# Layer norms whose last sums go through TensorE, with the high part taken from the affine step

## The chip, the cores and the metric

The kernel runs on one core of a Trainium2 chip. The metric is the device time of one execution in microseconds. Three runs of the kernel before took 2368.23, 2368.1 and 3208.11 us, median 2368.23.

## What is computed

The reference is a two-layer encoder over 256 tokens of width 1024. A layer has a mixing part (four mixers on one modulated input, gates, a projection) and an expert part, each closed by a layer norm on the scaled residual plus the gated result:

```python
mod = (c_act @ w_ada[l] + b_ada[l]).reshape(bsz, 6, 1, D_MODEL)
...
h = x * (1.0 + scale1) + shift1
...
mix = jnp.sum(gates * proj, axis=2) @ w_out[l]
x = layer_norm(ALPHA * x + gate1 * mix, ln_g[l, 0], ln_b[l, 0])
h2 = x * (1.0 + scale2) + shift2
y = peer_ffn(h2, p_wq[l], p_subkeys[l], p_u[l], p_v[l])
x = layer_norm(ALPHA * x + gate2 * y, ln_g[l, 1], ln_b[l, 1])
```

There are so four norms in the program: the first and the second norm of each of the two layers. The modulation `mod` is a product of one vector with a 1024 x 6144 matrix per layer.

## The kernel before

Nearly all work is a list of jobs, one per weight tile of 1024 x 128: 70 for the input projection of a layer, 16 for the branches, 8 for the output projection, 16 for the expert queries, 128 each for the two expert tables. SyncE's queue loads a tile (`raw`, three buffers). ScalarE copies it into a high part (`whi`, line 230), VectorE subtracts that from the tile and keeps the low part (`wlo`, line 233). TensorE then makes three matmuls for each of the eight chunks of 128 input features (lines 238 to 240), 24 per job, into a PSUM tile `main`, which rotates over three banks. A tile is split two jobs ahead of its use. Evictions, attention work, the scans of the recurrent mixer and other small work are put between the jobs. The Python code records the work in this order; within it a scheduler decides what stands where on each engine, except for calls through `VB` and `SB`, which stay in the order of the code.

**The norms.** The residual `r` lies feature-major, eight chunks of 128 features x 256 tokens (in the first norm of a layer it is part of the tile `mixA`). A token's mean and variance are sums over the 128 partitions and the eight chunks. `stats` is called for each chunk when it is there: ScalarE squares it (lines 297 and 301), VectorE adds the chunk to a running sum (line 303) and its square to another (line 307). In the first norm the last chunk, in the second the last two, are left out of the running sum and go to TensorE themselves. `norm` then has TensorE multiply each running sum with a column of ones (line 331, tile `lnst`), VectorE works out the mean and the reciprocal root by three Newton steps on two columns (lines 312 to 341), and TensorE spreads the result over all partitions with transposes (line 319, tile `lnb`). VectorE multiplies and adds (line 350) in groups of one or two chunks, one instruction per chunk and operation. `emit` makes the next layer's input of each chunk: an affine step on ScalarE with the norm's and the modulation's factors (`hf`, line 367), its high part by a copy (`hhi`, line 230), its low part on VectorE (`hlo`, line 233). Eight more affine steps on ScalarE (line 372, the folds) bring `r` itself up to date; four of them the scheduler puts between the emits. The norm's successor jobs can't begin before `hhi` and `hlo`. So the first three weight tiles behind a norm (areas) are loaded and split during the jobs before it (`areas_of`), and their 72 matmuls run chunk by chunk as the chunks come. Behind them on TensorE, in the first norms, stands a small product `ssc` (line 881), whose input is the first area job's result, evicted by ScalarE (`qf`, line 1028).

**The end of the expert part.** The second expert table is accumulated in four banks (`vacc`, lines 1084 to 1086), and the last three tiles are held back so that the banks finish one after the other. `take` copies a finished bank to SBUF (ScalarE line 1110, VectorE line 1108), `turn` transposes it on TensorE (`vt`, line 1119), and line 1156 adds it to `r`.

**The modulation.** In layer 0, the 24 halves of 512 KB that the rest of the layer needs are loaded between weight tiles into two rooms in `mixA` (`stage`), and VectorE multiplies and sums each (line 252, `staged`). Job numbers set when: a half is loaded at job 8i/3 and summed three jobs later.

**Scans.** The recurrent mixer works in two directions; each takes a square root on ScalarE (line 662), then gates and scans on VectorE.

## Time and profile before

| | us |
|---|---|
| median of three runs | 2368.23 |
| profiled execution | 2363.6 |
| its span in the trace | 2361.8 |
| TensorE busy | 2289.1 |
| VectorE busy | 1823.6 |
| ScalarE busy | 1262.6 |

The trace holds one execution. Times in its rows count from the start of the span. A row of the timeline gives the start, the time from the first start to the last end, engine, line, operation, destination and sources, shape and, behind an x, how many like instructions in a row it stands for; in square brackets stands how long the engine had been idle and what ended that. Loads of weights into TensorE (PEld) run beside its matmuls (PE). A line with SPq is an entry of SyncE's DMA queue.

### The profile page before, as it was taken

How to read it: one execution, taken by the hardware profiler on the slowest of the kernel's cores; microseconds unless marked ns; L12 is line 12 of the kernel's file. 1: busy time of each engine (PE TensorE's matmuls, PEld its weight loads, DVE VectorE, ACT ScalarE, POOL GpSimd, SP SyncE). 2: the span in 40 equal slices, each digit the busy share in tenths (PEclk: the TensorE clock that was granted, in tenths of full speed). 3: DMA queues.
4: the chain of work that ended last, by engine and by line, in shares of the span. 5: the costliest groups of instructions: out<-in, count | busy, mean ns of one | idle time of the engine just before them, and what ended most of it. 6: DMA issues, size and time to landing. Idle time of an engine off the chain costs nothing.

```text
span 2361.8 us, 43572 instructions
## 1 busy us (share of the span) xinstructions
PE 2289.1 (97%) x16488; PEld 2125.9 (90%) x16488; DVE 1823.6 (77%) x3929; ACT 1262.6 (53%) x2539; POOL 0.2 (0%) x4
## 2 busy tenths in 40 slices
PE   5999999999999999999989999999999999999997
PEld 4998898999999988888889999999999999888886
DVE  7887788998889777777766866889888896665555
ACT  5666546455554454545546765465555545445544
POOL 0000000000000000000000000000000000000000
PEclk9999999999999999999989999999999999999998
DMA  9665454454444577788744454545544445665563
GB/s 357 223 202 203 169 185 171 169 183 165 158 163 160 184 245 274 268 289 294 253 175 157 139 175 154 201 155 173 176 161 161 161 171 199 230 213 194 191 212 108
DMA packets 128033, 461.80 MB, mean 196 GB/s; under 512 B 15440, under 2 KB 20048, under 8 KB 124624
## 3 DMA queue, kind: packets, MB, share of 16 engines
q1 hardware_dynamic: 126816, 453.25, 55.1%
q10 hardware_dynamic: 1008, 5.77, 0.6%
q8 instruction: 131, 2.15, 0.4%
q14 instruction: 78, 0.64, 0.1%
HBM read 450.31 MB, written 5.24 MB: 193 GB/s over the span
## 4 chain that ended last, share of the span: by engine, by line
PE 81%; DVE 10%; DMA 4%; ACT 2%; issue 2%; SPq 0%; ACTq 0%; DVEq 0%
PE main L238 16%; PE main L239 15%; PE main L240 15%; PE vacc L1085 9%; PE vacc L1086 9%; PE vacc L1084 9%; DVE wlo L233 3%; DVE topk L93 2%; PE gw L996 1%; PE gw L997 1%; DMA raw<-in_w_in 1%; DMA mixA<-in_w_ada 1%; DMA adav<-in_w_ada 1%; DVE ada L252 1%; ACT whi L230 1%
## 5 line engine op out<-in xcount | busy, mean ns | idle before, releaser
L233 DVE TENSOR_TENSOR wlo<-raw,whi 128x1024 fp32r<-128x1024 f32 x723 | 879.4, 1218 | 308.3 <-ACT whi L230 305.9
L238 PE MATMUL main<-hhi,wlo 128*128 128x256 f32 x3456 | 1000.4, 290 | 3.7 <-DVE wlo L233 3.1
L240 PE MATMUL main<-hhi,whi 128*128 128x256 f32 x3456 | 978.9, 283 | 0.0
L239 PE MATMUL main<-hlo,whi 128*128 128x256 f32 x3456 | 978.4, 283 | 0.0
L230 ACT ACTIVATE whi<-raw 128x1024 fp32r<-128x1024 f32 x720 | 761.9, 1058 | 402.3 <-PE vacc L1086 278.8
L238 PEld LDWEIGHTS main<-hhi,wlo 128*128 128x128 f32 x3456 | 663.1, 192 | 9.2 <-DVE wlo L233 4.7
L239 PEld LDWEIGHTS main<-hlo,whi 128*128 128x128 f32 x3456 | 663.7, 192 | 0.5
L240 PEld LDWEIGHTS main<-hhi,whi 128*128 128x128 f32 x3456 | 663.1, 192 | 0.1
L1085 PE MATMUL vacc<-wlo,wv 128*128 128x512 f32 x1024 | 398.9, 390 | 0.5 <-DVE wlo L233 0.5
L1084 PE MATMUL vacc<-whi,wv 128*128 128x512 f32 x1024 | 398.6, 390 | 0.0
L1086 PE MATMUL vacc<-whi,wv 128*128 128x512 f32 x1024 | 398.5, 389 | 0.0
L1085 PEld LDWEIGHTS vacc<-wlo,wv 128*128 128x128 f32 x1024 | 192.2, 188 | 41.5 <-DVE wlo L233 1.9
L1084 PEld LDWEIGHTS vacc<-whi,wv 128*128 128x128 f32 x1024 | 192.1, 188 | 40.1 <-ACT whi L230 0.4
L1086 PEld LDWEIGHTS vacc<-whi,wv 128*128 128x128 f32 x1024 | 192.2, 188 | 39.9
L1053 ACT ACTIVATE gel<-main 128x256 f32<-128x256 f32 (+20 forms) x192 | 56.6, 295 | 298.5 <-PE main L240 298.5
L981 DVE TENSOR_TENSOR oha<-ohe,ijg 128x512 f16<-128x512 f16 x256 | 98.5, 420 | 0.9
L252 DVE CUSTOM_DVE_ANT_0 adav<-adav,cact,prm 128x1024 f32<-128x1024 f32 x56 | 71.8, 1283 | 32.4 <-DMA adav<-in_w_ada 31.8
L978 DVE TENSOR_TENSOR ohe<-iota,ijg 128x1024 f16<-128x1024 f16 x128 | 87.3, 683 | 0.2
L1056 DVE TENSOR_TENSOR GB<-GB,gel 128x256 f32<-128x256 f32 (+29 forms) x128 | 46.6, 364 | 45.8 <-ACT gel L1053 44.3
L238 PE MATMUL main<-mixB,wlo 128*128 128x256 f32 x256 | 73.3, 286 | 0.0
L240 PE MATMUL main<-mixB,whi 128*128 128x256 f32 x256 | 72.4, 283 | 0.0
L239 PE MATMUL main<-mixB,whi 128*128 128x256 f32 x256 | 72.4, 283 | 0.0
(233 smaller groups left out, 2215.8 us busy)
## 6 DMA issues: line engine op xcount, KB each, us to landing
raw<-in_p_u SPq DMA_DIRECT2D x256, 512.0 KB, 3.2
raw<-in_p_v SPq DMA_DIRECT2D x256, 512.0 KB, 4.3
raw<-in_w_in SPq DMA_DIRECT2D x134, 512.0 KB, 3.5
adav<-in_w_ada SPq DMA_DIRECT2D x56, 512.0 KB, 5.4
raw<-in_w_br SPq DMA_DIRECT2D x32, 512.0 KB, 3.2
raw<-in_p_wq SPq DMA_DIRECT2D x26, 512.0 KB, 3.3
mixA<-in_w_ada SPq DMA_DIRECT2D x24, 512.0 KB, 4.5
ada<-in_w_ada SPq DMA_DIRECT2D x8, 1024.0 KB, 15.7
```

The costliest lines, as they stand in the source:

```text
L230: return S.activation(hi, src, AF.Copy, scale=scale)
L233: return V.tensor_tensor(lo, src, hi.bitcast(F32), op=OP.subtract)
L238: PE.matmul(out, wlo(c), xhi(c), start=start and c == 0, stop=False)
L239: PE.matmul(out, whi(c), xlo(c), start=False, stop=False)
L240: PE.matmul(out, whi(c), xhi(c), start=False, stop=stop and c == n - 1)
L252: V.tensor_tensor_reduce(out=buf[:, k], in0=buf[:, k], in1=state["cact"], scale=1.0, scalar=prm[:, P_BADA + 48 * l + n:P_BADA + 48 * l + n ...
L978: V.tensor_tensor(flat(eq), iota16.rearrange("p (c k) -> p c k", k=2)[:, None].to_broadcast([128, 2 * NB, 64, 2]), twice(ijg[:, 0:2]), op= ...
L981: V.tensor_tensor(flat(a[:, i:i + 1]), flat(eq[:, 0:1]), ijg[:, 2 + i, :, None, :].to_broadcast([128, NB, 64, 2]), op=OP.mult)
L1053: S.activation(t[:, :n], out[:, :n], AF.Gelu_apprx_tanh)
L1084: PE.matmul(o, wl[:, tt], hi, start=first, stop=False)
L1085: PE.matmul(o, wh[:, tt], lo, start=False, stop=False)
L1086: PE.matmul(o, wh[:, tt], hi, start=False, stop=last)
```

## The change

1. `stats` keeps running sums for the first four chunks alone; chunks 4 to 7 and their squares go to TensorE as they are. The loop over the sums' matmuls now runs over the chunks first, and over sum and square inside.
2. VectorE multiplies and adds chunks 0 and 1 singly and the others in pairs of 128 x 512.
3. `emit` takes the high part from the affine step itself: ScalarE runs that step twice, once into `hhi`, once into `hf`. The folds stay in the order of the code, behind all emits.
4. The last expert bank is finished in two halves of 256 columns, the first copied by VectorE, the second by ScalarE.
5. For the queries' areas the loads are put two jobs earlier (`areas_of` with 2 for 4); splits of areas come two jobs and more behind the loads, where it was one.
6. Both square roots of the scans stay in the order of the code, one right behind the other.
7. Modulation halves are summed five jobs behind their load, where it was three.

```diff
-    def stats(r, m, direct):
+    def stats(r, m, end):
...
-            state["rs"] = [r]
+            state["rs"], state["sqs"] = [r], [state["ss"][:, 1]]
...
-        if m < NC8 - direct:
+        if m < NC8 // 2:
             V.tensor_tensor(ss[:, 0], state["rs"][0], r, op=OP.add)
             state["rs"] = [ss[:, 0]]
+            V.tensor_tensor(ss[:, 1], ss[:, 1], sq, op=OP.add)
         else:
             state["rs"].append(r)
-        state["stats_end"] = V.tensor_tensor(ss[:, 1], ss[:, 1], sq, op=OP.add)
+            state["sqs"].append(sq)
+        state["stats_end"] = end
...
-        for i, xs in enumerate((state["rs"], [state["ss"][:, 1]])):
-            for k, x in enumerate(xs):
+        n = len(state["rs"])
+        for k in range(n):
+            for i, xs in enumerate((state["rs"], state["sqs"])):
...
-        for ms in ((0,), (1, 2), (3, 4), (5, 6), (7,)):
+        for m0, m1 in ((0, 1), (1, 2), (2, 4), (4, 6), (6, 8)):
             for i, op in enumerate((OP.mult, OP.add)):
-                for m in ms:
-                    V.tensor_tensor(r[:, m], r[:, m], b[i], op=op)
-            for m in ms:
+                V.tensor_tensor(r[:, m0:m1], r[:, m0:m1], b[i][:, None].to_broadcast([128, m1 - m0, T]), op=op)
+            for m in range(m0, m1):
                 emit(m)
...
-            S.activation(h, r[:, m], AF.Identity, scale=fold[:, 0, 0, m:m + 1], bias=fold[:, 0, 1, m:m + 1])
-            marks["hi"] = split_hi(hi[:, m], h)
+            for a in (hi[:, m], h):
+                marks["hi"] = S.activation(a, r[:, m], AF.Identity, scale=fold[:, 0, 0, m:m + 1], bias=fold[:, 0, 1, m:m + 1])
...
-            S.activation(r[:, m], r[:, m], AF.Identity, scale=fold[:, 1, 0, m:m + 1], bias=fold[:, 1, 1, m:m + 1])
+            SB.activation(r[:, m], r[:, m], AF.Identity, scale=fold[:, 1, 0, m:m + 1], bias=fold[:, 1, 1, m:m + 1])
...
-            before[n + 1 + i].hooks.append(lambda i=i, j=j: area_split(i, j))
+            before[n + 2 + i].hooks.append(lambda i=i, j=j: area_split(i, j))
...
-                S.activation(tr, tr, AF.Sqrt)
+                SB.activation(tr, tr, AF.Sqrt)
...
-            w[8 * i // 3 + 3].hooks.append(lambda i=i: staged(i))
+            w[8 * i // 3 + 5].hooks.append(lambda i=i: staged(i))
...
-        areas_of(jobs[-16:], outs, 4)
+        areas_of(jobs[-16:], outs, 2)
...
-                        for i, x in enumerate(held):
-                            three(b, *x, False, i == VLAST - 1)
-                        take(b)
-                        if b:
-                            turn(b - 1)
+                        for part in ((0, 512),) if b < 3 else ((0, 256), (256, 256)):
+                            for i, x in enumerate(held):
+                                three(b, *x, False, i == VLAST - 1, *part)
+                            take(b, *part)
+                            if b and part[0] == 0:
+                                turn(b - 1)
                     turn(3)
```

On TensorE, at the first norm of layer 0, stands between the last output job's matmuls (`main0`) and the transposes of the result, before:

```order
L239 MATMUL main0_4260<-hlo_3403,whi_4188 128x256
L240 MATMUL main0_4260<-hhi_3402,whi_4188 128x256
L331 MATMUL lnst7_4303<-ones_87,lnss_4035 128x1 x2
L331 MATMUL lnst7_4303<-ones_87,mixA_241 128x1 x2
L331 MATMUL lnst7_4303<-ones_87,lnss_4035 128x1 x2
L319 MATMUL lnb6_4330<-cst_82,rs_4316 128x128 x2
```

and with the change, down to the sum and the square of chunk 4; the last two rows then stand three more times, for chunks 5 to 7:

```order
L239 MATMUL main0_4254<-hlo_3402,whi_4188 128x256
L240 MATMUL main0_4254<-hhi_3401,whi_4188 128x256
L334 MATMUL lnst7_4296<-ones_87,lnss_4035 128x1 x4
L334 MATMUL lnst7_4296<-ones_87,mixA_241 128x1 x2
L334 MATMUL lnst7_4296<-ones_87,sq_4186 128x1 x2
```

Six matmuls of the program have become twenty, all of them still behind the last output job. The first square's product stands third, ahead of all chunks' own.

On VectorE, at the second norm of layer 0, from the first sum that needs the last expert bank (`vt6`, `vt0` are its transposes, `lnss` the running sums) to the first rows that no longer belong to the sums, before:

```order
L1156 SCALAR_TENSOR_TENSOR r2_13314<-vt6_13695,gq_13705,r2_13314 128x256
L307 TENSOR_TENSOR lnss_13708<-lnss_13708,sq_13721 128x256
L303 TENSOR_TENSOR lnss_13708<-lnss_13708,r2_13314 128x256
L307 TENSOR_TENSOR lnss_13708<-lnss_13708,sq_13726 128x256
L1156 SCALAR_TENSOR_TENSOR r2_13314<-vt6_13695,gq_13705,r2_13314 128x256
L1156 SCALAR_TENSOR_TENSOR r2_13314<-vt0_13696,gq_13705,r2_13314 128x256
L303 TENSOR_TENSOR lnss_13708<-lnss_13708,r2_13314 128x256
L307 TENSOR_TENSOR lnss_13708<-lnss_13708,sq_13731 128x256
L1156 SCALAR_TENSOR_TENSOR r2_13314<-vt0_13696,gq_13705,r2_13314 128x256
L307 TENSOR_TENSOR lnss_13708<-lnss_13708,sq_13736 128x256
L434 MEMSET mixA_13849 128x4x2
L435 MEMSET mixA_13849 128x4
```

and with the change:

```order
L1158 SCALAR_TENSOR_TENSOR r2_13315<-vt6_13696,gq_13716,r2_13315 128x256
L303 TENSOR_TENSOR lnss_13719<-lnss_13719,r2_13315 128x256
L1158 SCALAR_TENSOR_TENSOR r2_13315<-vt6_13696,gq_13716,r2_13315 128x256
L305 TENSOR_TENSOR lnss_13719<-lnss_13719,sq_13722 128x256
L1158 SCALAR_TENSOR_TENSOR r2_13315<-vt0_13697,gq_13716,r2_13315 128x256
L305 TENSOR_TENSOR lnss_13719<-lnss_13719,sq_13727 128x256
L1158 SCALAR_TENSOR_TENSOR r2_13315<-vt0_13697,gq_13716,r2_13315 128x256
L305 TENSOR_TENSOR lnss_13719<-lnss_13719,sq_13732 128x256
L233 TENSOR_TENSOR wlo_13757<-raw_13595,whi_13756 128x512
L337 TENSOR_SCALAR lnw_13783<-lnst7_13762 128x2
```

Of seven plain adds (the seventh follows behind the two clears) four are left; three of these are for the squares of chunks 1 to 3, of which the first stood ahead of these rows before.

On ScalarE, at the first norm of layer 0, the last chunks' emits, the folds of `mixA` and the first evictions of the area jobs (`qf`), before:

```order
L367 ACTIVATE hf<-mixA,fold 128x256
L372 ACTIVATE mixA<-mixA,fold 128x256
L230 ACTIVATE hhi<-hf 128x256
L372 ACTIVATE mixA<-mixA,fold 128x256 x4
L1028 ACTIVATE qf<-main_4396 128x256
L373 DMA xd<-mixA 128x2048
```

and with the change:

```order
L370 ACTIVATE hhi<-mixA,fold 128x256
L370 ACTIVATE hf<-mixA,fold 128x256
L93 ACTIVATE mixA<-mixA,fold 128x256 x8
L1029 ACTIVATE qf<-main_4397 128x256
L375 DMA xd<-mixA 128x2048
L1029 ACTIVATE qf<-main_4424 128x256
```

All eight folds (line 93 is that of the helper that keeps the order) are now between the last emit and the first eviction; before, four stood among the emits. The copy into `hhi` is an affine step.

## Rows read from the trace of the kernel before

**Rows 1.** The page: busy time, share of the span, instructions.

```profile
PE 2289.1 (97%) x16488; PEld 2125.9 (90%) x16488; DVE 1823.6 (77%) x3929; ACT 1262.6 (53%) x2539; POOL 0.2 (0%) x4
```

**Rows 2.** Waits of TensorE: total us, times, longest.

```profile
PE lnst L331 <- DVE lnss L303: 5.3, 2, 2.9
...
PE z L652 <- DVE mixA L478: 2.7, 1, 2.7
```

**Rows 3.** Waits of VectorE.

```profile
DVE mixA L252 <- DMA mixA<-in_w_ada: 22.1, 13, 4.3
```

**Rows 4.** Busy time by window: length, engines, PEclk (granted clock), DMA share, GB/s.

```profile
60.00:310.00 250.00, 240.94 (x1907) 225.92 (x1906) 193.27 (x428) 151.72 (x315) 0.00 (x0) 0.99 0.57 198
1220.00:1470.00 250.00, 249.06 (x2018) 235.97 (x2017) 175.01 (x389) 157.69 (x321) 0.00 (x0) 1.00 0.48 163
...
270.00:280.00 10.00, 7.20 (x43) 7.00 (x42) 8.57 (x22) 5.11 (x14) 0.00 (x0) 0.76 0.44 159
```

**Rows 5.** Timeline of a late modulation half in layer 0: SyncE's queue, VectorE, TensorE.

```profile
262.60 1.40 SPq L247 DMA_DIRECT2D mixA<-in_w_ada  x1
...
268.61 1.28 DVE L252 CUSTOM_DVE_ANT_0 mixA<-mixA,cact,prm 128x1024 f32<-128x1024 f32 x1 [4.35 <-DMA mixA<-in_w_ada]
...
275.12 0.96 PE L620 MATMUL stc<-ones,sqc 128*128 128x1 f32 x4 [2.80 <-ACT sqc L616]
```

**Rows 6.** Timeline of TensorE, first norm of layer 0: the sums' matmuls.

```profile
373.34 0.51 PE L331 MATMUL lnst<-ones,lnss 128*128 128x1 f32 x4
...
375.05 0.61 PE L331 MATMUL lnst<-ones,lnss 128*128 128x1 f32 x4 [0.36 <-DVE lnss L307]
```

**Rows 7.** The same, second norm of layer 0.

```profile
1194.42 1.84 PE L331 MATMUL lnst<-ones,r 128*128 128x1 f32 x8
1196.13 0.99 PE L331 MATMUL lnst<-ones,lnss 128*128 128x1 f32 x4
```

**Rows 8.** Busy time by window around the two second norms' sums.

```profile
1193.00:1194.00 1.00, 0.45 (x3) 0.46 (x3) 1.00 (x4) 0.64 (x2) 0.00 (x0) 0.69 0.97 410
...
2346.00:2347.00 1.00, 0.88 (x8) 0.79 (x8) 0.87 (x3) 0.42 (x2) 0.00 (x0) 1.00 0.05 16
2347.00:2348.00 1.00, 0.92 (x6) 0.83 (x5) 0.85 (x2) 0.38 (x1) 0.00 (x0) 0.55 0.00 0
```

**Rows 9.** Groups of ScalarE in 380 to 391: count, busy us, mean ns, idle before.

```profile
L367 ACT ACTIVATE hf<-mixA,fold 128x256 f32<-128x256 f32 x8 | 4.5, 588 | 5.9 <-DVE mixA L350 5.9
L372 ACT ACTIVATE mixA<-mixA,fold 128x256 f32<-128x256 f32 x8 | 4.4, 587 | 0.0
L230 ACT ACTIVATE hhi<-hf 128x256 fp32r<-128x256 f32 x8 | 3.0, 403 | 0.0
```

**Rows 10.** Timeline behind the first norm of layer 0: first affine step, first eviction, ssc.

```profile
380.42 0.60 ACT L367 ACTIVATE hf<-mixA,fold 128x256 f32<-128x256 f32 x1 [5.88 <-DVE mixA L350]
...
390.90 0.36 ACT L1028 ACTIVATE qf<-main 128x256 f32<-128x256 f32 x1
...
391.52 0.61 PE L881 MATMUL ssc<-subk,qf 128*128 128x128 f32 x4
```

**Rows 11.** Timeline of the second norm of layer 0: scaled and plain adds, first eviction, fourth job.

```profile
1186.88 1.66 DVE L1156 SCALAR_TENSOR_TENSOR r<-vt,gq,r 128x256 f32<-128x256 f32 x4 [2.05 <-PE vt L1119]
...
1190.89 0.48 DVE L1156 SCALAR_TENSOR_TENSOR r<-vt,gq,r 128x256 f32<-128x256 f32 x1
...
1194.76 0.42 DVE L307 TENSOR_TENSOR lnss<-lnss,sq 128x256 f32<-128x256 f32 x1 [0.18 <-ACT sq L301]
...
1212.76 0.38 ACT L687 ACTIVATE mixA<-main 128x256 f32<-128x256 f32 x1 [0.24 <-PE main L240]
...
1213.52 0.28 PE L238 MATMUL main<-hhi,wlo 128*128 128x256 f32 x1
```

**Rows 12.** Timeline of the last norm: VectorE's last adds, the last sums' matmuls.

```profile
2347.02 0.96 DVE L307 TENSOR_TENSOR lnss<-lnss,sq 128x256 f32<-128x256 f32 x2 [0.15 <-ACT sq L301]
...
2348.04 1.01 PE L331 MATMUL lnst<-ones,lnss 128*128 128x1 f32 x4
```

More of the change, by code (lines that the diff above doesn't have):

```diff
@@ L327, in norm @@
         stp = bank(7, [128, 2, 2], name="lnst")
-        for i, xs in enumerate((state["rs"], [state["ss"][:, 1]])):
-            for k, x in enumerate(xs):
+        n = len(state["rs"])
+        for k in range(n):
+            for i, xs in enumerate((state["rs"], state["sqs"])):
                 for t in range(2):
-                    PE.matmul(stp[:, i, t:t + 1], x[:, t * 128:(t + 1) * 128], ones, start=i == k == t == 0, stop=k == len(xs) - 1,
+                    PE.matmul(stp[:, i, t:t + 1], xs[k][:, t * 128:(t + 1) * 128], ones, start=i == k == t == 0, stop=k == n - 1,
                               skip_group_check=True)
@@ L805, in post @@
                 r = state["r"][:, m]
-                V.scalar_tensor_tensor(r, out, mods[l][:, 16 + m:17 + m], r, op0=OP.mult, op1=OP.add)
-                stats(r, m, 1)
+                stats(r, m, V.scalar_tensor_tensor(r, out, mods[l][:, 16 + m:17 + m], r, op0=OP.mult, op1=OP.add))
             return Job(src=A["w_out"][l, m], mm=mm, post=post)
@@ L1077, in pre, with three @@
                 state["wv", j] = w[:, 0], w[:, 1]
-            def three(b, hi, lo, wh, wl, first, last):
-                o = state["acc4"][b]
+            def three(b, hi, lo, wh, wl, first, last, o0=0, n=512):
+                o = state["acc4"][b][:, o0:o0 + n]
                 tt = slice(b % 2 * 128, b % 2 * 128 + 128)
-                hi, lo = (x.rearrange("p c m -> p (c m)")[:, b // 2 * 512:b // 2 * 512 + 512] for x in (hi, lo))
-                PE.matmul(o, wl[:, tt], hi, start=first, stop=False)
-                PE.matmul(o, wh[:, tt], lo, start=False, stop=False)
-                PE.matmul(o, wh[:, tt], hi, start=False, stop=last)
+                hi, lo = (x.rearrange("p c m -> p (c m)")[:, b // 2 * 512 + o0:b // 2 * 512 + o0 + n] for x in (hi, lo))
+                PE.matmul(o, wl[:, tt], hi, start=first, stop=False, skip_group_check=o0 > 0)
+                PE.matmul(o, wh[:, tt], lo, start=False, stop=False, skip_group_check=o0 > 0)
+                PE.matmul(o, wh[:, tt], hi, start=False, stop=last, skip_group_check=o0 > 0)
             def mm(hi, lo):
@@ L1103, in layer, with take @@
         held = []
-        def take(b):
-            out = state["raws"][:, NAREA * D + 512 * b:NAREA * D + 512 * (b + 1)]
-            if b % 2:
-                V.tensor_copy(out, state["acc4"][b])
+        def take(b, o0, n):
+            out, acc = state["raws"][:, NAREA * D + 512 * b + o0:NAREA * D + 512 * b + o0 + n], state["acc4"][b][:, o0:o0 + n]
+            if b % 2 and o0 == 0:
+                V.tensor_copy(out, acc)
             else:
-                S.activation(out, state["acc4"][b], AF.Copy)
+                S.activation(out, acc, AF.Copy)
         def turn(b):
@@ L1155, in ln2 @@
             for m in range(NC8):
-                V.scalar_tensor_tensor(r[:, m], state["turned", m // 4][m % 4 // 2][:, m % 2], gq[:, m:m + 1], r[:, m],
-                                       op0=OP.mult, op1=OP.add)
-                stats(r[:, m], m, 2)
+                stats(r[:, m], m, V.scalar_tensor_tensor(r[:, m], state["turned", m // 4][m % 4 // 2][:, m % 2], gq[:, m:m + 1],
+                                                         r[:, m], op0=OP.mult, op1=OP.add))
             g, b = pv(P_LNG + 16 * l + 8, 8), pv(P_LNB + 16 * l + 8, 8)
```

## Prediction

> **What bounds the kernel now.** I read the page first: TensorE is busy for 97% of the span [rows 1], so an edit on another engine moves the time only where TensorE waits for that engine. Next the list of waits, sorted by engine. For TensorE it names the norms (the sums' matmuls wait 5.3 us for VectorE's adds, in two places) and the mixing of layer 0 (z waits 2.7 us) [rows 2]; for VectorE it names a DMA wait of 22.1 us in front of the modulation sums [rows 3]. The third view is busy time by window. It shows what these mixing waits are worth, because layer 1 runs the same mixing jobs without modulation sums: of 250 us TensorE is busy for 240.94 in layer 0 and for 249.06 in layer 1 [rows 4], so 8.1 us more stand idle in layer 0. Then the timeline of the places that the change touches. The median of the runs before is 2368.2 us and the profiled execution took 2363.6; I work out a difference in the profiled execution and add it to the median.
>
> **Part one: sums in the norms.** Before, the sums' matmuls come in two places at the layer-0 first norm: four at 373.34, when the last output job's matmuls are just done, and the last four from 375.05 on, ending at 375.66 (375.05 + 0.61) [rows 6]. Between them TensorE waits for VectorE. One matmul of the program is two on the chip (six make twelve). Four take 0.51, of which the last is 0.17 long: (0.51 - 0.17) / 3 = 0.11 us from one to the next, though each has a single column. The change makes 20 of the program, 40 on the chip, and the order puts all of them behind the last job's matmuls. 39 x 0.11 + 0.2 = 4.5 us from 373.34 is 377.8: 2.2 us later than now. VectorE's two adds that are saved were worth less than the matmuls that replace them. The first norm of layer 1 is laid out in the same way: 2.2 again.
>
> In the second norms VectorE was the limit: behind the last bank's transposes stand four scaled adds and seven plain adds, from 1190.89 to 1195.18 (1194.76 + 0.42) [rows 11]. In the new order four of each stand there. Four scaled adds take 1.66 [rows 11], about 0.41 each; a plain add starts about 0.34 after its predecessor in the same stretch ((1195.18 - 1190.89 - 1.66 - 0.3 of a wait and two clears) / 7). The bank's first half is ready before the second and feeds the first two scaled adds, so I let them start at about 1190.1. That gives 1190.1 + 1.66 + 4 x 0.34 = 1193.1 (0.8 later if they start as now). But the last of VectorE's adds gates the fifth of 40 matmuls: 36 are still to come. What these take hangs on TensorE's clock. At full clock 36 x 0.11 = 4.0, end 1197.1: no change against now (1196.13 + 0.99 = 1197.12) [rows 7]. At half clock eight took 1.84 [rows 7], 0.21 from one to the next: 7.7, end 1200.9, +3.8. The granted clock fell to 1.2 GHz between 1193 and 1194 (0.69 of full as a mean), with TensorE less than half busy; in the last norm it fell at about 2347.1, with these one-column matmuls in flight [rows 8]. So I expect the fall about a microsecond into the run: 8 at 0.11, 28 at 0.21, end about 1200.2, +3.1. In the last norm, by the same steps, the adds end at about 2345.8 in place of 2347.98 (2347.02 + 0.96), and 10 at 0.11 with 26 at 0.21 end at 2352.6 against 2349.05 [rows 12]: +3.5 (+0.8 at full clock).
>
> A rule speaks to that. Rows 7 and 8 show eight and then four sums' matmuls back to back at half clock, and no rise. The Trainium skill (TensorE: Matmul & The Clock Gate, section "What's actually happening") says that the slow clock is the default and "activity releases the throttle"; a longer run of matmuls might then keep the clock up. By the rows the two second norms cost 3.1 and 3.5; by the rule they would cost 0 and 0.8. No row here has 40 of them in one run, so the rule is a rival below.
>
> **Part two: the high part straight from the affine step, folds behind.** The first high chunk comes 0.4 us earlier, one ScalarE copy less. But ScalarE's total grows. Before: eight affine steps, eight copies, eight folds, which fill 10.48 us from 380.42 to the query eviction at 390.90 that TensorE's next matmuls (ssc, 391.52) need [rows 10]. A copy is 0.403 long against 0.588 for an affine step or fold [rows 9]. The change turns the eight copies into affine steps: 8 x 0.18 = 1.4 us more. The paired adds of VectorE bring chunk 2 some 0.4 later than now, when two single adds would do. So the eviction comes about 1.75 later, and TensorE stood at it with next to no slack (the eviction ends at 391.26, ssc starts at 391.52). Putting the folds last doesn't help, since the eviction stands behind all eight in either order. With 0.1 to 0.3 of slack I take +1.5 in each first norm. In layer 0's second norm the first eviction (1212.76) was just in time for the fourth job at 1213.52 [rows 11]; ScalarE was free 0.24 earlier, at 1212.52; with the folds 1.75 later the eviction ends at 1212.52 + 1.75 + 0.38 = 1214.65: +1.1. The last norm has no such step; pairs save VectorE about 0.5 there.
>
> **Part three: last bank in halves.** Twice nine matmuls of half the width cost TensorE about the same; the second half waits for VectorE's copy of the first, which mostly lies beside the four transposes placed between. It is in the 1190.1 above; alone 0 to +0.3.
>
> **Part four: areas' loads two places earlier, splits one later.** The weights arrive long before their use either way; 0, since no row shows TensorE waiting for a raw load here. If that cover failed, one load's landing would show, once per layer.
>
> **Part five: both square roots in a row.** Fewer table loads on ScalarE (18 in the new order, 22 before), beside TensorE's matmuls: 0. The first direction's scan work moves later into the gate jobs, where VectorE has more to do: 0 to +2, I take +1 in layer 0 and 0 in layer 1.
>
> **Part six: modulation sums two jobs later.** At 262.60 a half is loaded, at 268.61 VectorE has waited 4.35 us for it, and TensorE's stc at 275.12 waits 2.80 [rows 5]; the granted clock over 270 to 280 is 0.76 [rows 4], so about 4.8 us ran at half clock, worth 2.4. With z's 2.7 [rows 2] that is 7.9 from below the counter. Two jobs are about 5.8 us, more than the longest wait. From both sides: 0, if the waits come back elsewhere, and 8.1 + 2.4 = 10.5, if all of layer 0's idle time goes. I take 6.5, since the scans and the first jobs also make some of the idle time.
>
> **Sum.** First norms 2 x (2.2 + 1.5) = 7.4; second norm of layer 0 3.1 + 1.1 = 4.2; last norm 3.5 - 0.5 = 3.0; scans +1; modulation sums -6.5. Together +9.1, so 2372.7 in the profiled execution and 2377 as a median.
>
> **Rivals.** First, the clock stays up through the sums: the second norms cost 1.1 and 0.3 in place of 4.2 and 3.0, the sum is +3.3: 2371.5. For it: in the last norm eight of the sums' matmuls ran at full clock before it fell. Against it: in layer 0 the clock was down before the second eight began. Second, the later sums remove nothing, since a half's next load now stands on SyncE's queue behind the sum of the half before it in two jobs of three, and raw weight loads queue behind that: +15.6, 2384. Against it: at 262.60 the load was issued only 1.65 us before VectorE came to the sum (268.61 - 4.35), so VectorE is ahead of the queue and the new wait is mostly met already. Third, on the other side: the DMA waits of VectorE count in full, because in layer 0 the mixing is a chain through VectorE and each wait pushes all that follows. Then 22.1 [rows 3] goes and the sum is 7.4 + 4.2 + 3.0 + 1 - 22.1 = -6.5: 2361.7, not slower. It decides as soon as the mixing gives more than the 15.6 that the rest costs. Against it: only 8.1 us more are idle in layer 0 than in layer 1 [rows 4].
>
> **How the numbers follow.** The forecast 0.5 (its own range 2372 to 2383), the clock that stays up 0.2, sums that give nothing 0.15, the full gain of the mixing 0.1; 0.05 for what I don't see. The range of 8 in 10 reaches from the third rival to a little beyond the second: 2362 to 2387. A measurement of this kernel tells about 2% from no change, 47 us here; no case comes near that on either side, so within 2% gets 0.97, slower 0.02, faster 0.01.
>
> **What would show it.** In the profile after: 40 sums' matmuls per norm; the first broadcast of the layer-0 first norm 2 us later behind the last output job; the first query eviction 3.5 to 4 us later behind that job, with a TensorE wait for ssc of over a microsecond; the second norms' sums at 0.21 from one to the next for most of the run; no VectorE wait of over 2 us for a modulation half. I am wrong if the sums' matmuls run closer than 0.11, if they begin before the last job's end, if ScalarE is not what the job behind the areas waits for, or if layer 0's mixing gains more than 10 us or nothing.

## The result and the profile after

The changed kernel took 2379.71 us as a median of five runs (2378.36 to 2383.85). The kernel before took 2363.14 to 2368.23 us in four of five runs; the fifth, of 3208 us, is left aside. The ratio is 1.0064 with an interval of 1.0053 to 1.0075, so the change costs 12 to 18 us. The prediction was 2377 us, with +9.1 over the kernel before; it added this to 2368.2 us, and the four runs here have a median of 2366.2. The profiled execution took 2379.28 us, 15.7 more than the profiled one of before.

VectorE's wait for the sums' matmuls in the kernel before (total, times, longest):

```profile
DVE lnw L334 <- PE lnst L331: 2.5, 2, 1.4
```

The page and the waits of the changed kernel, beside [rows 1 to 3]:

```profile
PE 2307.4 (97%) x16610; PEld 2145.1 (90%) x16610; DVE 1810.9 (76%) x3879; ACT 1262.4 (53%) x2537; POOL 0.2 (0%) x4
```

```profile
PE main L238 <- DVE wlo L233: 7.2, 8, 2.4
...
PE ssc L882 <- ACT qf L1029: 1.9, 2, 1.2
PE lnst L334 <- DVE lnss L305: 1.6, 1, 1.6
...
DVE lnw L337 <- PE lnst L334: 19.8, 4, 6.6
...
DVE mixA L252 <- DMA mixA<-in_w_ada: 17.4, 10, 4.2
```

TensorE's wait for the sums' adds has shrunk from 5.3 us to 1.6; VectorE's wait for the sums' matmuls has grown from 2.5 us to 19.8. The wait has changed sides. A wait of `ssc` for ScalarE is new, and the wait for modulation halves is 17.4 us in 10 places, where it was 22.1 in 13 [rows 3].

The timeline at the first norm of layer 0, TensorE and ScalarE, to be read beside [rows 6, 10]. The first broadcast before:

```profile
378.51 1.12 PE L319 MATMUL lnb<-cst,rs 128*128 128x128 f32 x4 [2.86 <-DVE rs L316]
```

and the changed kernel:

```profile
369.49 0.95 PE L334 MATMUL lnst<-ones,lnss 128*128 128x1 f32 x8
...
373.43 0.58 PE L334 MATMUL lnst<-ones,sq 128*128 128x1 f32 x4
376.86 1.11 PE L321 MATMUL lnb<-cst,rs 128*128 128x128 f32 x4 [2.85 <-DVE rs L318]
...
387.09 4.04 ACT L93 ACTIVATE mixA<-mixA,fold 128x256 f32<-128x256 f32 x8
391.03 0.36 ACT L1029 ACTIVATE qf<-main 128x256 f32<-128x256 f32 x1
...
391.44 0.71 PE L882 MATMUL ssc<-subk,qf 128*128 128x128 f32 x4 [0.65 <-ACT qf L1029]
```

From the first sums' matmul to the broadcast it is 376.86 - 369.49 = 7.37 us; before, 378.51 - 373.34 = 5.17. All eight folds stand in front of the eviction, and TensorE waits for it: it begins 391.03 - 376.86 = 14.17 us behind the broadcast, before 390.90 - 378.51 = 12.39.

The second norm of layer 0, timeline and windows, beside [rows 7, 8]:

```profile
1192.53 0.61 PE L334 MATMUL lnst<-ones,lnss 128*128 128x1 f32 x4 [1.57 <-DVE lnss L305]
...
1198.63 0.99 PE L334 MATMUL lnst<-ones,sq 128*128 128x1 f32 x4
```

```profile
1192.00:1193.00 1.00, 0.47 (x5) 0.47 (x5) 1.00 (x3) 0.42 (x1) 0.00 (x0) 1.00 0.84 352
1193.00:1194.00 1.00, 1.00 (x9) 1.00 (x8) 0.07 (x1) 0.00 (x0) 0.00 (x0) 0.69 1.04 442
1194.00:1200.00 6.00, 5.62 (x27) 5.53 (x26) 0.34 (x5) 0.00 (x0) 0.00 (x0) 0.50 0.48 199
```

The 36 matmuls behind VectorE's last add begin at 1192.53; the clock falls to 1.2 GHz a microsecond later and stays there, with TensorE busy for 5.62 of 6 us.

One stretch was not in the forecast, the first jobs of layer 1. `wblk` is a weight tile of the mixing that is loaded there; its entry follows that of the residual's store 3.9 to 4.2 us later in every trace. Before:

```profile
1216.71 0.33 SPq L432 DMA_DIRECT2D wblk<-in_d_w  x1
1217.13 2.41 SPq L1199 DMA_DIRECT2D raw<-in_w_in  x3
...
1222.89 1.06 ACT L230 ACTIVATE whi<-raw 128x1024 fp32r<-128x1024 f32 x1 [3.02 <-DMA raw<-in_w_in]
```

After:

```profile
1217.11 0.39 PE L238 MATMUL main<-hhi,wlo 128*128 128x256 f32 x1 [0.49 <-ACT mixA L689]
...
1220.80 0.33 SPq L434 DMA_DIRECT2D wblk<-in_d_w  x1
1221.21 2.86 SPq L1200 DMA_DIRECT2D raw<-in_w_in  x3
...
1228.85 1.06 ACT L230 ACTIVATE whi<-raw 128x1024 fp32r<-128x1024 f32 x1 [5.29 <-DMA raw<-in_w_in]
...
1231.22 0.58 PE L238 MATMUL main<-hhi,wlo 128*128 128x256 f32 x1 [2.32 <-DVE wlo L233]
```

Raw loads stand on SyncE's queue behind that of `wblk`, which stands behind the residual's store, and the store waits for the folds. Counted from the start of TensorE's fourth job (1213.52 before [rows 11], 1217.11 now), the three raw loads are issued 3.6 us later before and 4.1 now; the copy of the first follows 5.8 us behind the issue before and 7.6 now, and TensorE stood still for 2.3 us. So the late folds account for about 0.5 us of the delay, and the loads' own time for 1.9.

The stretches below are worked out from the starts of the first instruction of each group in seven traces (one execution each): the kernel before, the changed one, and experiments that follow. "Fourth job" is the first TensorE work behind the 72 area matmuls.

| stretch, us | before | changed | e1 | e2 | e5 | e7 | e9 |
|---|---|---|---|---|---|---|---|
| mixing, layer 0 | 356.1 | 352.4 | 356.8 | 360.0 | 357.7 | 352.1 | 354.1 |
| norm 1: sums to broadcast | 5.2 | 7.4 | 5.3 | 7.6 | 5.2 | 5.2 | 5.2 |
| broadcast to fourth job | 13.0 | 14.6 | 14.6 | 13.4 | 14.2 | 14.2 | 12.4 |
| norm 2: first transposes to broadcast | 16.1 | 19.6 | 15.9 | 19.8 | 16.1 | 15.9 | 15.4 |
| broadcast to fourth job | 13.5 | 14.5 | 14.6 | 13.7 | 13.1 | 13.2 | 12.4 |
| mixing, layer 1 | 313.6 | 317.2 | 314.0 | 312.8 | 313.6 | 313.1 | 312.7 |
| norm 1, layer 1: sums to broadcast | 5.2 | 7.9 | 5.2 | 7.4 | 5.2 | 5.3 | 5.3 |
| broadcast to fourth job | 13.0 | 14.6 | 14.6 | 14.0 | 14.3 | 14.5 | 12.4 |
| last norm: first transposes to broadcast | 15.5 | 18.7 | 16.4 | 15.9 | 15.8 | 16.3 | 16.0 |

The mixing of layer 0 shows how far single executions can be trusted: the changed kernel, e1 and e2 run the same code there and differ by 7.6 us. The stretch from a broadcast to the fourth job varies too: e5, e11 and e12, with the emits of before, took 13.1 to 14.4 us there, where the trace of before has 13.0 to 13.5. The last norm varies with the clock: e2 has the sums of the changed kernel and took 15.9 us in place of 18.7, and e6 took 16.1.

### The profile page after: what moved, and what is told of

The parts are those of the page before. It is cut to its first block, busy times and chain, and to the rows that moved or that the text cites. A ratio compares the mean times of both kernels' runs of the same rounds, so it can differ in the third digit from the quotient of the medians.

```text
span 2377.4 us, 43769 instructions
## 1 busy us (share of the span) xinstructions
PE 2307.4 (97%) x16610; PEld 2145.1 (90%) x16610; DVE 1810.9 (76%) x3879; ACT 1262.4 (53%) x2537; POOL 0.2 (0%) x4
## 4 chain that ended last, share of the span: by engine, by line
PE 87%; DVE 6%; ACT 3%; DMA 3%; issue 1%; SPq 0%; ACTq 0%; DVEq 0%
PE main L238 17%; PE main L239 17%; PE main L240 17%; PE vacc L1085 10%; PE vacc L1087 10%; PE vacc L1086 10%; DVE wlo L233 2%; PE gw L997 1%; DMA mixA<-in_w_ada 1%; PE gw L998 1%; PE lnst L334 1%; DVE ada L252 1%; PE ssc L882 1%; PE pt L507 1%; DMA raw<-in_w_in 1%
## 5 line engine op out<-in xcount | busy, mean ns | idle before, releaser
L238 PEld LDWEIGHTS main<-hhi,wlo 128*128 128x128 f32 x3456 | 664.7, 192 | 14.5 <-DVE wlo L233 9.3
L1085 PE MATMUL vacc<-whi,wv 128*128 128x512 f32 (+1 forms) x1030 | 400.2, 389 | 0.2
L1086 PE MATMUL vacc<-wlo,wv 128*128 128x512 f32 (+1 forms) x1030 | 400.0, 388 | 0.0
L1087 PE MATMUL vacc<-whi,wv 128*128 128x512 f32 (+1 forms) x1030 | 399.8, 388 | 0.0
```

The source lines that it names most:

```text
L238: PE.matmul(out, wlo(c), xhi(c), start=start and c == 0, stop=False)
L1085: PE.matmul(o, wl[:, tt], hi, start=first, stop=False, skip_group_check=o0 > 0)
L1086: PE.matmul(o, wh[:, tt], lo, start=False, stop=False, skip_group_check=o0 > 0)
L1087: PE.matmul(o, wh[:, tt], hi, start=False, stop=last, skip_group_check=o0 > 0)
```

## The experiments

Each ratio is to runs of the kernel before on the same chip. Where a run is set against the changed kernel or another experiment, it is by medians. The changed kernel was timed apart from all experiments, and e5 to e8 on another chip than e1 to e4 and e9 to e12; so the difference of the two ratios is given where it tells another story.

**e1, the first part taken back.**

```diff
-        if m < NC8 // 2:
+        if m < NC8 - direct:
...
-            state["sqs"].append(sq)
+        state["stats_end"] = V.tensor_tensor(ss[:, 1], ss[:, 1], sq, op=OP.add)
```

> The changed kernel with its first part taken back: running sums on VectorE for all but one chunk in the first norms and all but two in the second, squares all on VectorE, 12 and 16 sums' matmuls on the chip. Theory: the 40 matmuls cost 2.2 and 2.7 us in the first norms, 3.5 in layer 0's second and 3.2 in the last, 11.6 together, and come back in full; about 2368 median, 0.995 of the changed kernel, and about 4 us above the fast runs of the kernel before. Rival: VectorE's saved adds were worth something and the loss lies in the emits and what follows; then under 5 us come back (2375 or more).

Measured: 2367.84 us, ratio 1.0003 (0.9989 to 1.0017): 11.9 us below the changed kernel. The three stretches from sums or transposes to broadcast that belong to layers 0 and 1 are back at 5.3, 15.9 and 5.2. The sums' matmuls are the greatest part of the loss; by the two ratios it is 14 us.

**e2, folds on VectorE.**

```diff
-            SB.activation(r[:, m], r[:, m], AF.Identity, scale=fold[:, 1, 0, m:m + 1], bias=fold[:, 1, 1, m:m + 1])
+            V.tensor_scalar(r[:, m], r[:, m], fold[:, 1, 0, m:m + 1], fold[:, 1, 1, m:m + 1], op0=OP.mult, op1=OP.add)
```

> The changed kernel with the eight folds on VectorE in place of ScalarE. Theory: the late folds hold the first eviction in each norm (0.5 to 0.8 us of TensorE's wait) and, in layer 0's second norm, the store of the residual, behind which the room of wblk and with it the raw loads of layer 1 wait (2.3 us of wait and about 1.7 by the clock that falls); both go: about 4 to 6 us less than the changed kernel, 2374 to 2376, and no wait of TensorE for wlo at the start of layer 1. Rival: the stall at the start of layer 1 comes from another thing (the splits of the areas one job later); then it stays and 1 to 2 us are saved.

Measured: 2374.48 us, ratio 1.0035 (1.0025 to 1.0046): 5.2 us below the changed kernel. The wait for `ssc` is gone in both first norms, and so is the one at the start of layer 1: the store comes 11.1 us behind the broadcast in place of 14.3, and in SyncE's queue a raw load now stands ahead of `wblk`.

```profile
1222.79 0.33 SPq L1200 DMA_DIRECT2D raw<-in_w_in  x1
1225.45 0.33 SPq L434 DMA_DIRECT2D wblk<-in_d_w  x1
1226.74 3.21 SPq L1200 DMA_DIRECT2D raw<-in_w_in  x2
```

So the folds on ScalarE held back `ssc`. For the start of layer 1 this run doesn't show the cause, because the loads stand in another order; e6 bears on it. The splits of the areas, one job later in this kernel too, don't make the stall by themselves.

**e3, the sums twice.** The second set goes into columns that nobody reads.

```diff
+        for k in range(n):
+            for i, xs in enumerate((state["rs"], state["sqs"])):
+                for t in range(2):
+                    PE.matmul(stp[:, 2 + i, t:t + 1], xs[k][:, t * 128:(t + 1) * 128], ones, start=False, stop=k == n - 1,
...
```

> The changed kernel with every norm's 40 sums' matmuls issued a second time into columns of the same bank that nobody reads. Theory: a sums' matmul costs 0.11 us at full and 0.21 at half clock and does not bring the clock back; the first norms cost between 4.5 (all at full) and 8.5 more each, the second norms 8.5 more each: 26 to 34 us, 2405 to 2414. Rival (a long run of matmuls keeps or brings the clock up): 4.5 each or less, since the first 40 would be faster too: 18 us or less, 2398 or less.

Measured: 2414.32 us, 34.6 above the changed kernel, just over the theory's end. Timeline and windows of the first norm of layer 0:

```profile
374.63 0.58 PE L334 MATMUL lnst<-ones,mixA 128*128 128x1 f32 x4
...
378.49 1.84 PE L339 MATMUL lnst<-ones,lnss 128*128 128x1 f32 x8
...
384.46 0.99 PE L339 MATMUL lnst<-ones,sq 128*128 128x1 f32 x4
```

```profile
374.00:378.00 4.00, 4.00 (x37) 4.00 (x38) 1.08 (x2) 0.42 (x1) 0.00 (x0) 0.99 0.02 4
378.00:380.00 2.00, 2.00 (x12) 2.00 (x11) 0.00 (x0) 0.00 (x0) 0.00 (x0) 0.50 0.00 0
380.00:382.00 2.00, 2.00 (x11) 2.00 (x11) 0.00 (x0) 0.00 (x0) 0.00 (x0) 0.50 0.00 0
382.00:386.00 4.00, 4.00 (x21) 4.00 (x20) 0.00 (x0) 0.00 (x0) 0.00 (x0) 0.50 0.00 0
```

Eighty one-column matmuls run back to back; TensorE is busy in every slice, and yet the clock falls to half after about the first forty and does not come back. The Trainium skill (TensorE: Matmul & The Clock Gate, section "What's actually happening") says that activity releases the throttle; this trace doesn't agree for one-column matmuls, and the measurement decides. Here a long run of sums neither kept the clock up nor brought it back, against the first rival of the prediction. But the fall doesn't come at the same place each time. In the last norm of e2, with the 40 sums from 2357.36 on, the clock held for most of the run:

```profile
2359.00:2361.00 2.00, 2.00 (x20) 2.00 (x19) 0.21 (x1) 0.72 (x2) 0.00 (x0) 1.00 0.03 8
2361.00:2363.00 2.00, 1.60 (x9) 1.51 (x9) 0.33 (x3) 0.00 (x0) 0.00 (x0) 0.54 0.00 0
```

That norm took 15.9 us there, 0.4 more than before, in place of the changed kernel's 3.2 more. So for single norms the rival can come true.

**e4, running sums last.**

```diff
-        for k in range(n):
+        for k in [*range(1, n), 0]:
```

> The changed kernel with the sums' matmuls in another order: the four late chunks and their squares first, the two running sums last. Theory: in the second norms 36 of 40 matmuls stood behind VectorE's last add; now 24 to 28 of them run while VectorE works, and the sums end 3 to 5 us earlier there; the first norms stay, as TensorE comes to them late: 6 to 9 us less than the changed kernel, 2371 to 2374. Rival (the number of matmuls at half clock decides, not what they wait for): under 2 us.

Measured: 2378.35 us, ratio 1.0056 (1.0033 to 1.0079), 1.4 below the changed kernel: a miss. In layer 0's second norm the stretch from the transposes to the broadcast fell from 19.6 to 16.7, as expected. In the last norm it stayed at 19.1: the sums now wait for the first late chunk itself,

```profile
2355.99 0.60 PE L334 MATMUL lnst<-ones,r 128*128 128x1 f32 x4 [1.48 <-DVE r L1158]
```

and the clock fell about a microsecond after, so nearly all ran at half speed. The first norm of layer 0 lost what the second gained: from the first sum to the broadcast it took 9.1 us in place of 7.4, with the granted clock at 0.50 from 374 on, in the middle of its sums. So what the order saves is less than what hangs on the moment at which the clock falls.

**e5, only the later modulation sums, on the kernel before.**

```diff
-            w[8 * i // 3 + 3].hooks.append(lambda i=i: staged(i))
+            w[8 * i // 3 + 5].hooks.append(lambda i=i: staged(i))
```

> The kernel before with one edit: the modulation halves of layer 0 summed five jobs behind their load in place of three. Theory (the prediction's): layer 0's mixing loses its waits, 4 to 6.5 us less than the kernel before, ratio 0.9973 to 0.9983. Rival (the second of the prediction): a later sum only makes the next load of the same room later, VectorE waits as often, and the time is that of the kernel before within 2 us, ratio 0.999 to 1.001. In the profile the two differ in VectorE's wait for halves: under 8 us against about 17 to 22.

Measured: ratio 0.9987 (0.9977 to 0.9997); medians 2364.77 and 2367.72 us. The gain is about 3 us, half of what the prediction took. VectorE waits for halves just as often:

```profile
DVE mixA L252 <- DMA mixA<-in_w_ada: 21.3, 12, 4.0
```

The trace shows why, and it is not the rival's reason. Here is the half of [rows 5] in this run, SyncE's queue and VectorE:

```profile
265.92 0.43 SPq L247 DMA_DIRECT2D mixA<-in_w_ada  x1
...
271.59 1.28 DVE L252 CUSTOM_DVE_ANT_0 mixA<-mixA,cact,prm 128x1024 f32<-128x1024 f32 x1 [4.02 <-DMA mixA<-in_w_ada]
```

The sum begins 5.7 us behind the issue of its load; before, it was 268.61 - 262.60 = 6.0. It has not moved. Counted by the tile splits (`wlo`) that stand ahead of it on VectorE, 23 of the 24 sums are where they were in the kernel before; only the fourth, at 85.7 before and 93.9 here, is one split further back. SyncE's queue has the same order in both traces. So the edit changed the job numbers in the Python code, and the scheduler put nearly all sums back where they had stood. The rooms were not the limit either: a load is issued 4.7 us or more after the sum that frees its room, in both traces. Where the 3 us come from is open: layer 0's mixing in the one trace is not shorter than before.

**e6, the emits as before**, on the changed kernel: `hhi` copied from `hf`, folds placed by the scheduler.

```diff
-            for a in (hi[:, m], h):
-                marks["hi"] = S.activation(a, r[:, m], AF.Identity, scale=fold[:, 0, 0, m:m + 1], bias=fold[:, 0, 1, m:m + 1])
+            S.activation(h, r[:, m], AF.Identity, scale=fold[:, 0, 0, m:m + 1], bias=fold[:, 0, 1, m:m + 1])
+            marks["hi"] = split_hi(hi[:, m], h)
...
-            SB.activation(r[:, m], r[:, m], AF.Identity, scale=fold[:, 1, 0, m:m + 1], bias=fold[:, 1, 1, m:m + 1])
+            S.activation(r[:, m], r[:, m], AF.Identity, scale=fold[:, 1, 0, m:m + 1], bias=fold[:, 1, 1, m:m + 1])
```

> The changed kernel with the third part taken back: the high part is copied from the affine step's result, and the scheduler places the folds. Theory: ScalarE's longer work behind the norms cost 1.6 us in each first norm, about 1 in layer 0's second and up to 3.6 at the start of layer 1, where raw loads stand behind a room that the stored residual frees: 4 to 7 us less than the changed kernel, about 2374, much as with the folds on VectorE. Rival: the first high chunk's 0.5 us is worth as much as the longer chain costs; then it is within 2 us of the changed kernel.

Measured: 2380.44 us, ratio 1.0046 (1.0033 to 1.0059). By medians that is 0.7 us above the changed kernel, as the rival had it; by the ratios it is 4 below, as the theory had it. The six runs spread from 2374.52 to 2386.50, so this doesn't decide. In its trace the fourth job comes without a wait for ScalarE, but the first area matmul comes 3.35 us after the broadcast, where it was 2.50, so a part of what is saved behind is spent in front.

The start of layer 1 is of more use. The store stands 12.6 us behind the broadcast again (before 12.7, changed 14.3), and the raw loads are issued 3.3 us behind the start of the fourth job. Yet TensorE stood still:

```profile
1229.58 3.25 SPq L1200 DMA_DIRECT2D raw<-in_w_in  x3
...
1238.08 1.06 ACT L230 ACTIVATE whi<-raw 128x1024 fp32r<-128x1024 f32 x1 [5.45 <-DMA raw<-in_w_in]
...
1240.45 0.58 PE L238 MATMUL main<-hhi,wlo 128*128 128x256 f32 x1 [2.48 <-DVE wlo L233]
```

The copy came 8.5 us after the issue. In e1, with the folds late, it came 5.8 us after, and TensorE's wait was 0.5 us. So the late folds are not what makes the stall large; the time of the loads is.

**e7, sums as before and folds on VectorE**: the diffs of e1 and e2 together.

> The changed kernel with the first part taken back (running sums on VectorE as before) and the folds on VectorE. Theory: both gains add, 11.9 and 5.2 us, since one lies ahead of the broadcast and the other behind it: about 2362.6, 0.998 to 0.999 of the kernel before. Rival: with VectorE free of folds again or the sums back, VectorE's queue delays the low parts; then 2366 or more.

Measured: 2363.63 us, ratio 0.9982 (0.9973 to 0.9991). The two gains add to 16 of the expected 17 us, and this is 4 us faster than the kernel before.

**e8, squares of the last chunks to TensorE as well**, on e7: 16 matmuls in the first norms, 24 in the second.

```diff
-        state["stats_end"] = V.tensor_tensor(ss[:, 1], ss[:, 1], sq, op=OP.add)
+            state["stats_end"] = V.tensor_tensor(ss[:, 1], ss[:, 1], sq, op=OP.add)
         else:
             state["rs"].append(r)
+            state["sqs"].append(sq)
```

> As the run before, but the chunks that the kernel before left out of the running sum (one in the first norms, two in the second) go to TensorE with their squares, 16 and 24 matmuls; in the second norms the running sums come last. Theory: one plain add less stands behind the last chunk and few matmuls are added, 0.5 us less in each first norm and about 1 in each second one: 2 to 3 us below the run before. Rival: 8 more matmuls at half clock cost the second norms 1.7 us each, no gain.

Measured: 2366.71 us, ratio 0.9999 (0.9990 to 1.0008), 3 above e7 in the same series: the rival. In the traces the two second norms, with eight matmuls more each, took 17.0 and 18.4 us from the first transposes to the broadcast, in e7 15.9 and 16.3. Even eight more of these matmuls cost what the saved adds bring and more.

**e9, idle TensorE filled around the norms**, on e7. The matmuls go into a bank that nobody reads.

```diff
+                PE.matmul(out, a[:, 0], a.rearrange("p c m -> p (c m)")[:, :512], start=True, stop=True)
...
+        warm(12, last_sum)
...
+        warm(8, last_b)
...
+            if b == 3:
+                warm(8, last_t)
```

> The fastest kernel so far (sums as before, folds on VectorE) with idle TensorE filled around the first three norms: 8 matmuls of 512 columns on area weights into an unread bank behind the last transposes of layer 0's second norm, 12 behind the sums of each norm, 8 behind each broadcast. Theory: behind a norm 72 matmuls take 10.7 to 11.9 us, of which 8.6 (72 at 0.12) is full clock; if TensorE never stands still the clock stays at 2.4 GHz, the areas take about 9, the broadcast 0.5 less and 16 sums' matmuls of layer 0's second norm 1.6 less: 7 to 10 us below that kernel, about 2355, 0.995 of the kernel before. Rival: the chain of affine steps and low parts paces the areas anyway; then under 3 us.

Measured: 2359.94 us, ratio 0.9977 (0.9964 to 0.9989). That is 3.7 below e7 by medians, but e7 was timed on another chip, and by the ratios it is 1 us, with intervals that overlap; a gain over e7 is not shown. Windows at the first norm, e7:

```profile
378.00:380.00 2.00, 1.94 (x9) 1.95 (x10) 2.00 (x5) 1.62 (x4) 0.00 (x0) 0.50 0.02 6
380.00:382.00 2.00, 2.00 (x11) 2.00 (x11) 2.00 (x6) 2.00 (x5) 0.00 (x0) 0.50 0.00 0
```

and e9, windows and timeline:

```profile
375.00:379.00 4.00, 3.98 (x20) 2.78 (x19) 3.83 (x15) 0.90 (x2) 0.00 (x0) 1.00 0.21 48
379.00:389.00 10.00, 9.35 (x75) 8.94 (x75) 9.74 (x24) 8.80 (x18) 0.00 (x0) 1.00 0.18 73
```

```profile
373.34 2.97 PE L330 MATMUL warm<-areas 128*128 128x512 f32 x12
376.33 0.69 PE L320 MATMUL lnb<-cst,rs 128*128 128x128 f32 x4
```

The clock stays up, and the fourth job comes 12.4 us after the broadcast in all three norms, in e7 13.2 to 14.5. But TensorE is busy for only 9.35 of 10 us there, with VectorE and ScalarE at 9.74 and 8.80. That fits the rival, by which these two pace the areas, and the gain is in any case under the theory's 7 us. This kernel has the lowest median of all that were run.

**e10, the same filling in the changed kernel**: the diff of e9.

> The changed kernel with the same filling. Theory: layer 0's second norm's 40 sums run at full clock and cost 3 us less, and the broadcasts 0.5 each; but the first eviction stays bound to ScalarE's 24 affine steps (24 x 0.49 = 11.8 us), so TensorE's faster areas end in a longer wait for it: 4 to 6 us below the changed kernel, 2374 to 2376. Rival: the loss of the changed kernel is the clock alone; then it falls to the kernel before or below, 2368 or less.

Measured: 2384.99 us, ratio 1.0076 (1.0060 to 1.0091), 5 us above the changed kernel, 3 by the ratios: a miss. Timeline of the second norm of layer 0:

```profile
1203.70 4.31 PE L332 MATMUL warm<-areas 128*128 128x512 f32 x12
1207.84 0.60 PE L322 MATMUL lnb<-cst,rs 128*128 128x128 f32 x4
...
1222.11 0.39 PE L238 MATMUL main<-hhi,wlo 128*128 128x256 f32 x1 [1.88 <-ACT mixA L702]
```

The sums ran at full clock (it had fallen at their very end), but then the twelve filling matmuls ran at half clock, took 4.31 us in place of the 2.97 in e9, and held up the broadcast. That was this experiment's own doing. Its last row shows the other half of the theory: the 72 area matmuls took 9.8 us in place of 11.3, and the wait for ScalarE's eviction grew from 0.5 to 1.9 us.

**e11, only the bank in halves**, and **e12, only the square roots**, both on the kernel before.

```diff
-                        for i, x in enumerate(held):
-                            three(b, *x, False, i == VLAST - 1)
+                        for part in ((0, 512),) if b < 3 else ((0, 256), (256, 256)):
+                            for i, x in enumerate(held):
+                                three(b, *x, False, i == VLAST - 1, *part)
```

```diff
-                S.activation(tr, tr, AF.Sqrt)
+                SB.activation(tr, tr, AF.Sqrt)
```

> The kernel before with one edit: the last expert bank in halves. Theory: VectorE reaches the last chunks a little earlier, but is itself the limit up to the end of the sums: 0 to 1 us less, ratio 0.9993 to 1.0003. Rival: the wait of the second half for VectorE's copy of the first costs as much as it brings or more; ratio above 1.0003.

> The kernel before with one edit: both square roots in the order of the code. Theory: table loads lie beside TensorE's work and four fewer bring nothing; the scans of the first direction come later and crowd VectorE: 0 to 2 us more, ratio 1.000 to 1.001. Rival: four table loads of 1.28 us count; 3 to 5 us less, ratio 0.998 to 0.9987.

Measured: 1.0005 (0.9994 to 1.0015) for the halves, 0.9991 (0.9980 to 1.0002) for the roots. Neither can be told from no change. For the halves the interval holds nearly all of the theory's range and a part of the rival's. For the roots it holds the whole of the rival's range, 3 to 5 us less, and of the theory's only the edge at no change; the medians differ by 3.6 us. So the roots lean to the rival, without being clear of noise.

## Why the prediction was right, and where it was not

**The sums, +2.2, 2.2, 3.1 and 3.5.** Right, in mechanism and size: 2.2, 2.7, 3.5 and 3.2 us in the profile, and 11.9 in e1 against the 11.0 of the forecast. In layer 1's first norm the clock fell within the run, hence 2.7. The single prices are not fixed, since they hang on when the clock falls: the last norm cost 3.2 us here, but 0.4 in e2 and 0.6 in e6, which have the same sums.

**The clock.** The forecast that it falls about a microsecond into the run held in both second norms of the changed kernel. e3 shows that a run of sums doesn't bring it back; in the last norm of e2 and e6 it held for most of the run, as the first rival had it.

**ScalarE behind the norms, +1.5, 1.5 and 1.1.** The mechanism held: the eviction begins 1.78 us later behind the broadcast, forecast 1.75, and the fourth job comes 14.5 to 14.6 us behind it in all three norms of the changed kernel and of e1, e3 and e4, which have the same emits. Against the one trace of before that is 1.6, 1.1 and 1.6 longer. But that trace was a quick one: over before, e5, e11 and e12 the stretch is 13.8, 13.6 and 13.7 as a mean, so the cost is nearer 0.8, 1.0 and 0.9, an estimate from four executions. The prediction took TensorE's side of the sum, the time of the 72 area matmuls, as fixed; they took 9.9 us before and 11.2 in the changed kernel in the first norm of layer 0, and in e5, with the emits of before, 11.0 and 11.1 in the first norms. That part hangs on when the clock comes back in the one execution.

**The last norm's -0.5 for pairs.** Not seen: from its broadcast to the end the kernel took 9.95 us, before 9.81.

**The modulation sums, -6.5.** The step that failed is "modulation sums two jobs later": the sums did not come two jobs later. In e5 23 of 24, and in the changed kernel 22 of 24, stand behind as many tile splits on VectorE as before, and VectorE still came to many of them before their data. It waited 17.4 us in the changed kernel and 21.3 in e5, against 22.1; the longest wait was 4.2 us, where the prediction looked for none over 2. So the place in the Python code, which the prediction read, was not the place on the engine. e5 measured 3 us all the same, and their source is open. The prediction called itself wrong if layer 0's mixing gained nothing; eleven traces with this part took 352.1 to 360.6 us there, 355.9 as a mean, and the three without it, before, e11 and e12, 356.1, 360.9 and 354.4. A gain of a few us is possible; these traces don't show one. The second rival, by which the next load of a room stands behind the later sum, is not what happened either, since the loads came 4.7 us or more after those sums.

**The areas' loads and "no row shows TensorE waiting for a raw load": 0.** Wrong in place, though small. The late folds delayed the store of the residual, and with it the queue of raw loads at the start of layer 1, by about 0.5 us against TensorE's work. Where the loads took as long as before (e1), that made a wait of 0.5 us; the 2.3 us in the profiled execution came with loads that took 7.6 us, and e6 has 2.5 us with the folds as before and 8.5. In e1, e3 and e4 the stretch was 0.5 to 1.5 longer than before, in the changed kernel 3.6.

**Halves, 0, and roots, 0 with +1 for the scans.** e11 doesn't contradict the first. e12, which moves the roots and with them the scans, gave 0.9991 (0.9980 to 1.0002): the +1 us lies outside, and a gain of 3 to 5 us, from fewer table loads or from the other order, lies within.

The sum of +9.1 came out 3 to 9 us too low. It was near partly by luck: -6.5 stands in it for a move that hardly took place, and the terms behind the norms are too high by about 1.4 us, as they came from one quick execution. What the experiments show in place of the sum is 11.9 us for the sums (e1), 5.2 that go when the folds leave ScalarE (e2), and, with both put right, a kernel that is 4.1 us faster than before (e7). Together 13.0, where the medians of the changed kernel and of before differ by 13.6.

## What to carry to other kernels

Before moving adds from a waiting engine to TensorE, count what the moved work costs there in instructions and weights loaded: 24 to 28 more one-column matmuls per norm cost more than the adds that they replaced, and each takes 0.21 us in place of 0.11 once the clock has fallen. Where a scheduler orders the instructions, look at the order on the engine before and after an edit: here the scheduler kept nearly all sums of the modulation where they were, and one of the seven changes hardly took place. When work is put last on an engine, follow the buffer that it frees: here eight folds held a store, the store a room, and the room a queue, which was worth about 0.5 us. A gain that is read from the idle time of one execution needs the spread of that stretch over several before it is put in a sum.

## What was not expected of the hardware

TensorE's clock fell to half while the engine was busy without a gap: in e3 the windows from 374 to 386 show it busy throughout, at 0.99 and then 0.50. With 512-column matmuls in the waits of that norm (e9) it stayed at 1.00. Busy time in a profile does not say that the clock will hold.

A load's time decided a stall. From the issue of the raw loads behind `wblk`, at the start of layer 1, to the first copy it took 5.8 us in the kernel before and in e1, 7.6 in the changed kernel and 8.5 in e6; TensorE waited 0, 0.5, 2.3 and 2.5 us. Why the loads were slower in two of these executions is open.
